# One fp32 product for the mean square, its eps folded into the sums; two products of constants at the start

## The chip, the cores and the metric

One core of a Trainium2 chip runs the kernel. The metric is the device time of one execution in microseconds (us). Five engines work side by side, each in its own order: TensorE (PE; its weight loads are listed as PEld), VectorE (DVE), ScalarE (ACT), GpSimd (POOL) and SyncE (SP), which here only issues DMAs.

## The reference

A layer over 2048 tokens of width 1024, all float32:

```python
h = rmsnorm(x, g_attn); p = h @ w_in            # 1024 x 2816
y_a = a_b * conv3(a_c * a_h)                    # 256 wide
y_b = silu(layernorm(conv31(glu) + b_conv_b))   # 256 wide
y_c = stick_breaking_attention(q, k, v)         # 8 heads of 64
x = x + concat(y_a, y_b, y_c) @ w_out
x = x + relu(rmsnorm(x, g_ffn) @ w_ff1)**2 @ w_ff2   # 4096 wide
return rmsnorm(x, g_final)

def rmsnorm(x, g):
    return x * rsqrt(mean(x * x, -1) + 1e-6) * g
```

## The kernel before, in words

Everything is kept transposed: features on the 128 partitions, tokens along the free dimension, in blocks of TB = 512 tokens. Each large product is made of three (`mm3`): operands are split into a rounded high part and a rest, high x high, rest x high and high x rest are summed in PSUM. The splits are made on ScalarE (the high part) and VectorE or GpSimd (the rest).

First part: `consts` and `attention_consts` fill constant tiles, among them `d1` (128x512, zeros with a one in every 32nd column, two fills on VectorE, lines 195 and 196), and load `g_attn`. `p_start` then loads the first 512 tokens of x and the first two units of `w_in`, and multiplies them as they come: for each of the 8 pieces d, `make_h` loads x, makes the high part `xh` (ScalarE, line 229) and the rest `xl` (VectorE, line 230), squares the piece (`x_square`: ScalarE, then an add on VectorE into `ss`) and yields; the two units' weights are split every second d; then the products of this d are issued (lines 317 to 319). After the first block `vectors` loads seven small vectors on SP's queue, `norm_x` makes R, the reciprocal root of the mean square spread over the partitions, and the results leave PSUM multiplied by R (`p_evac`, line 341 for the first). The second block of 512 tokens follows in the same way with one unit, and then `p_half` twice with all units, `mixer_b` and the first attention groups woven in.

Second part: four times `block`, one for each 512 tokens. It multiplies by w_out and adds x (`x2`), keeping `acc` (8 tiles), `hh` and `hl` (acc times g_ffn, split) and `ss`, the sum of squares. The FFN is computed on the values that are not yet normalised, so that its result has to be divided by the mean square m (plus eps); instead `acc` is multiplied by m and the last norm, which doesn't depend on a common factor, has its eps multiplied by m squared. For that `block` sums `ss` over the partitions with four fp32 products into a `z` bank (`colsum`, `ps_ss`), makes `mt` and `em` on VectorE, spreads `mt` over the partitions with four more fp32 products (`spread`, `ps_R`), and multiplies the eight `acc` tiles (line 1008). In the profile an fp32 product is two records. After that `ffn1` and `ffn2` alternate (32 pieces and 8 groups), the last group's results are squared into `ss2` (`square_sum`), and `finish_` makes the last norm from `ss2` with `em` as its eps. Attention of the next 512 tokens is woven into the first three blocks; its score tiles (`ps_z`, line 528) share the three `z` banks, and its chain on VectorE ends at T (line 656), on whose result further products wait. In the last block the final group runs in two halves of 256 tokens, and the first half's `finish_` is put into the second.

A planner orders the instructions of each engine's queue: it walks the program in its order, with some parts at higher priority (`high_priority`), and uses its own estimates of when each can start.

Of the kernel before, what the change touches and what calls it, by code (L numbers as in the profile page):

```python
# [7 lines left out]
F32 = mybir.dt.float32  # L8
F32R = mybir.dt.float32r
I32 = mybir.dt.int32  # L10
AF = mybir.ActivationFunctionType
# [4 lines left out]
P = 128  # L16
# [12 lines left out]
RMS_EPS = 1e-6  # L29
LN_EPS = 1e-5  # L30

UNITS = ["G0", "G1", "A0", "A1", "A2", "K0", "K1", "Q0", "Q1", "V0", "V1"]


def f(ap):
    return ap.bitcast(F32)
# [32 lines left out]
class Trunk:  # L69
# [39 lines left out]
    def rsqrt(self, ss, scale, eps, cols=slice(0, 4)):  # L109

        nc, pool = self.nc, self.tiny
        y = pool.tile([P, 4], F32, name="rs_y", tag="rs_y", bufs=6)
        v = pool.tile([P, 4], F32, name="rs_v", tag="rs_v")[:, cols]
        if isinstance(eps, float):
            nc.vector.tensor_scalar(v, ss[:, cols], scale, eps, op0=ALU.mult, op1=ALU.add)
        else:
            nc.vector.scalar_tensor_tensor(v, ss[:, cols], scale, eps[:, cols], op0=ALU.mult, op1=ALU.add)  # L117
        nc.gpsimd.tensor_tensor(y[:, cols], v, self.mhalf[:, cols], op=ALU.pow)  # L118
        return y
# [23 lines left out]

    def small(self, name, bufs=2):
        return self.tiny.tile([P, 4], F32, name=name, tag=name, bufs=bufs)


    def consts(self, ctx):
        nc, tc, a = self.nc, self.tc, self.a
        c = self.c = ctx.enter_context(tc.tile_pool(name="consts", bufs=1))  # L150
        self.tiny = ctx.enter_context(tc.tile_pool(name="tiny", bufs=2))
        self.dr = ctx.enter_context(tc.tile_pool(name="dr", bufs=1, space=DRAM))
        self.gvec = {}
        t = c.tile([P, DC], F32, name="g_attn")
        nc.scalar.dma_start(t, a["g_attn"].rearrange("(d p) -> p d", p=P))
        self.gvec["g_attn"] = t

        self.ident = c.tile([P, P], F32, name="ident")
        make_identity(nc, self.ident)
        self.ones2 = c.tile([P, 2], F32, name="ones2")  # L160
        nc.vector.memset(self.ones2, 1.0)
        self.mhalf = c.tile([P, 4], F32, name="mhalf")
        nc.vector.memset(self.mhalf, -0.5)
        self.KQ = self.dr.tile([H // 2, 2, P, 3, 2, S // 2], F32, name="KQ")
        self.VS = self.dr.tile([H, S, 2 * HD], F32, name="VS")
        self.Y = self.dr.tile([D, S], F32, name="Y")

        self.WS = self.dr.tile([len(UNITS), 2, P, DC, 256], F32, name="WS")


        self.split_w = {n: self.dr.tile([k, 2, P, 2, DC // 2, P], F32, name="s_" + n) for n, k in (("w_out", DC), ("w1", FC))}
        self.split_w["w2"] = self.dr.tile([FC // G, DC // 2, P, 2, G, 2, P], F32, name="s_w2")

    def vectors(self):
        nc, tc, a, c = self.nc, self.tc, self.a, self.c
        self.vb = {}
        for name in ("g_ffn", "g_final"):
            t = c.tile([P, DC], F32, name=name)
            self.dma(t, a[name].rearrange("(d p) -> p d", p=P))
            self.gvec[name] = t  # L180
        c = self.pc
        self.wa = c.tile([P, 2, 3], F32, name="wa")
        self.dma(self.wa, a["w_conv_a"].rearrange("(c p) k -> p c k", p=P))
        self.wb = c.tile([P, 2, 31], F32, name="wb")
        self.dma(self.wb, a["w_conv_b"].rearrange("(c p) k -> p c k", p=P))
        for name in ("b_conv_b", "ln_b_g", "ln_b_b"):
            t = c.tile([P, 2], F32, name=name)
            self.dma(t, a[name].rearrange("(c p) -> p c", p=P))
            self.vb[name] = t
# [27 lines left out]
    def make_h(self, hf, tb):  # L217

        nc = self.nc
        g = 2 * hf + tb  # L220
        ss = self.mx.tile([P, TB], F32, name="ss", tag="ss", bufs=2) if hf == 0 else None
        for d in range(DC):
            t = self.rp.tile([P, TB], F32, name="xraw", tag=self.rt, bufs=self.rb)
            self.dma(t, self.a["xT"][d * P : (d + 1) * P, g * TB : (g + 1) * TB])
            gv = self.gvec["g_attn"][:, d : d + 1]
            hi = self.xp.tile([P, TB], F32R, name=f"xh{tb}_{d}", tag=f"xh{tb}", bufs=DC)
            lo = self.xp.tile([P, TB], F32R, name=f"xl{tb}_{d}", tag=f"xl{tb}", bufs=DC)
            self.xh[tb][d], self.xl[tb][d] = hi, lo
            nc.scalar.activation(hi, t, AF.Copy, scale=gv)
            nc.vector.scalar_tensor_tensor(lo, t, gv, f(hi), op0=ALU.mult, op1=ALU.subtract)  # L230
            if hf == 0:
                self.x_square(ss, t, d, nc.vector)
            yield d
        if hf == 0:
            self.ss[g] = ss
# [67 lines left out]
    def p_start(self):  # L303

        nc = self.nc
        ws = [self.w_steps(0), self.w_steps(1)]
        for tb, units in ((0, (0, 1)), (1, (0,))):
            xs = self.make_h(0, tb)
# [523 lines left out]

    def square_sum(self, ss, t, d):
        nc = self.nc
        if d == 0:
            nc.scalar.activation(ss, t, AF.Square)
# [17 lines left out]
    def block(self, tb, before):  # L854
# [107 lines left out]
        def ffn2(g, cols=slice(0, TB), ahead=0, again=0):  # L962
# [13 lines left out]
            for d in range(DC):  # L976
# [12 lines left out]
                elif g == FC // G - 1:  # L989
                    self.square_sum(ss2[:, cols], acc[d][:, cols], d)  # L990
                yield 0.65 * G
# [4 lines left out]
        need2(1)  # L996

        mt = self.small("mt")
        nc.vector.tensor_scalar(mt, self.colsum([ss], "z"), 1.0 / D, RMS_EPS, op0=ALU.mult, op1=ALU.add)
        em = self.small("em")  # L1000
        nc.vector.scalar_tensor_tensor(em, mt, RMS_EPS, mt, op0=ALU.mult, op1=ALU.mult)
        yield from ffn1(2)
        need2(2)
        ms = self.spread(mt, "z")
        for d in range(DC):
            if d == DC // 2:
                yield from ffn1(3)
            nc.vector.tensor_tensor(acc[d], acc[d], ms, op=ALU.mult)
        ss2 = hp.tile([P, TB], F32, name="ss2", tag="ss", bufs=1)
        sq7 = []  # L1010
# [8 lines left out]
        if tb < 3:  # L1019
            self.attend(tb + 1)  # L1020
            self.y_load(tb + 1, self.y_order(tb + 1)[: self.xb])
            yield from ffn2(FC // G - 1, ahead=2)
            self.end = self.finish_(tb, acc, [ss2], em)
        else:

            left, right = slice(0, TB // 2), slice(TB // 2, TB)
            yield from ffn2(FC // G - 1, left)
            fin = self.finish_(tb, acc, [ss2], em, left)
            with self.tc.high_priority(offset=HP):
                for n, _ in enumerate(ffn2(FC // G - 1, right, again=1)):  # L1030
                    for _ in range(LEFT[n]):
                        next(fin, None)
            self.finish(tb, acc, [ss2] + sq7, em, right)
            for _ in fin:
# [6 lines left out]

    def finish_(self, tb, acc, sums, em, cols=slice(0, TB)):
        nc, a, hp = self.nc, self.a, self.hp
        ts = slice(tb * TB + cols.start, tb * TB + cols.stop)
        bs = range(cols.start // P, cols.stop // P)
        b = slice(bs[0], bs[-1] + 1)
        y = self.rsqrt(self.colsum(sums, "z", bs), 1.0 / D, em, b)
        yield
# [106 lines left out]
```

## Time and profile before

| what | us |
|---|---|
| median of 3 runs | 2396.55 (2396.35 to 2400.49) |
| the profiled execution's own time | 2399.65 |
| its span, first to last instruction | 2397.6 |
| TensorE busy | 2372.1 (99%) |
| VectorE, ScalarE, GpSimd busy | 1513.9, 1066.5, 1138.9 |

Rows of the profile give the start and the length of an instruction or of a run of them ("x8"). TensorE's matmuls overlap each other, so that the distance from one start to the next says more than the length. "Idle before" in square brackets is how long the engine had waited and what ended it.

### The profile page before, as it was taken

To read this page: it belongs to the slowest core of one execution; us is meant where nothing else is said; L and a number is where in the kernel's file an instruction comes from. 1 tells how busy PE (TensorE), PEld (TensorE's weight loads), DVE (VectorE), ACT (ScalarE), POOL (GpSimd) and SP (SyncE) were. 2 spreads that over 40 slices of the span, in tenths; PEclk is the share of its full clock that TensorE was granted. 3 is DMA by queue.
4 is the path that set the end of the run, shared out by engine and by line. 5 is a ranking of instruction groups with operands and counts; after the bars stand their busy time and mean duration, and the time that the engine had idled before them with its cause. 6 is when DMAs were issued, how large, how long until landed. Compare 5 with 4: busy or idle time off the path is not lost.

```text
span 2397.6 us, 32859 instructions
## 1 busy us (share of the span) xinstructions
PE 2372.1 (99%) x11316; PEld 2003.4 (84%) x11316; DVE 1513.9 (63%) x2500; ACT 1066.5 (44%) x2002; POOL 1138.9 (48%) x1223
## 2 busy tenths in 40 slices
PE   8999999999999999999999999999999999999998
PEld 7888988898887888888888888788888888888887
DVE  7966698833878777768766668586666625322114
ACT  5232443333566566545555555355555522311221
POOL 1342397732576666526666665278878710000000
PEclk9999999999999999999999999999999999999999
DMA  7569897789687777696676876766676556545545
GB/s 253 209 229 344 292 324 237 258 258 279 187 238 214 221 216 214 199 286 180 214 226 221 241 240 206 267 172 179 193 202 197 181 176 224 181 166 194 205 168 193
DMA packets 236677, 532.28 MB, mean 222 GB/s; under 512 B 26848, under 2 KB 100576, under 8 KB 221152
## 3 DMA queue, kind: packets, MB, share of 16 engines
q1 hardware_dynamic: 178000, 457.82, 57.0%
q0 software_dynamic: 39424, 62.93, 11.8%
q10 hardware_dynamic: 19088, 9.44, 1.4%
q8 instruction: 89, 1.46, 0.3%
q14 instruction: 76, 0.62, 0.1%
HBM read 381.99 MB, written 139.72 MB: 218 GB/s over the span
## 4 chain that ended last, share of the span: by engine, by line
PE 86%; DMA 5%; DVE 3%; issue 3%; POOL 2%; ACT 1%; SPq 0%; POOLq 0%; DVEq 0%; ACTq 0%
PE ps_y L103 9%; PE ps_y L105 9%; PE ps_y L107 9%; PE ps_u L107 9%; PE ps_u L103 9%; PE ps_u L105 9%; PE ps_p L107 4%; PE ps_p L105 4%; PE ps_p L103 4%; PE ps_z L528 3%; PE ps_z L529 3%; PE ps_o L735 2%; PE ps_o L734 2%; PE ps_o L726 2%; PE ps_x L103 2%
## 5 line engine op out<-in xcount | busy, mean ns | idle before, releaser
L90 POOL TENSOR_TENSOR Alo<-A,Ahi 128x512 fp32r<-128x512 f32 x288 | 385.1, 1346 | 101.0 <-ACT Ahi L88 68.1
L984 DVE TENSOR_TENSOR acc<-acc,ps_y 128x512 f32<-128x512 f32 (+1 forms) x264 | 175.8, 668 | 188.4 <-PE ps_y L107 186.4
L103 PE MATMUL ps_u<-hh,w 128*128 128x512 f32 x1024 | 280.0, 392 | 2.5 <-ACT hh L903 2.4
L103 PE MATMUL ps_y<-fh,w 128*128 128x512 f32 (+1 forms) x1056 | 281.7, 384 | 0.0
L105 PE MATMUL ps_y<-fh,w 128*128 128x512 f32 (+1 forms) x1056 | 280.3, 383 | 0.0
L107 PE MATMUL ps_y<-fl,w 128*128 128x512 f32 (+1 forms) x1056 | 279.4, 383 | 0.0
L623 POOL TENSOR_TENSOR A<-A,R 128x512 f32<-128x512 f32 x168 | 223.8, 1335 | 115.4 <-ACT A L621 93.8
L105 PE MATMUL ps_u<-hh,w 128*128 128x512 f32 x1024 | 277.5, 390 | 0.0
L107 PE MATMUL ps_u<-hl,w 128*128 128x512 f32 x1024 | 277.1, 390 | 0.0
L118 POOL TENSOR_TENSOR rs_y<-rs_v,mhalf 128x4 f32<-128x4 f32 (+1 forms) x13 | 13.2, 1018 | 482.3 <-DVE rs_v L117 437.0
L948 ACT ACTIVATE ps_u<-ps_u 128x512 f32<-128x512 f32 x128 | 74.5, 582 | 353.6 <-PE ps_u L107 349.0
L105 PEld LDWEIGHTS ps_y<-fh,w 128*128 128x128 f32 x1056 | 195.0, 188 | 39.6 <-DMA w<-wraw 0.3
L107 PEld LDWEIGHTS ps_y<-fl,w 128*128 128x128 f32 x1056 | 195.0, 188 | 38.9 <-DVE fl L958 0.2
L105 PEld LDWEIGHTS ps_u<-hh,w 128*128 128x128 f32 x1024 | 192.2, 188 | 40.5
L107 PEld LDWEIGHTS ps_u<-hl,w 128*128 128x128 f32 x1024 | 191.9, 188 | 39.9
L103 PEld LDWEIGHTS ps_y<-fh,w 128*128 128x128 f32 x1056 | 193.2, 188 | 36.8 <-DVE acc L984 0.2
L88 ACT ACTIVATE Ahi<-A 128x512 fp32r<-128x512 f32 x288 | 176.8, 625 | 105.2 <-PE ps_o L734 44.9
L103 PEld LDWEIGHTS ps_u<-hh,w 128*128 128x128 f32 x1024 | 187.6, 188 | 37.9 <-ACT hh L903 3.4
L958 DVE TENSOR_TENSOR fl<-ps_u,fh 128x512 fp32r<-128x512 f32 x128 | 87.9, 687 | 205.3 <-ACT fh L957 204.7
L90 DVE TENSOR_TENSOR w<-wraw,w 128x512 fp32r<-128x512 f32 x184 | 186.0, 1036 | 30.9 <-ACT w L88 29.8
L625 DVE TENSOR_TENSOR R<-ps_z,R 128x512 f32<-128x512 f32 x168 | 115.7, 689 | 129.3 <-ACT ps_z L622 105.2
L88 ACT ACTIVATE w<-wraw 128x512 fp32r<-128x512 f32 x184 | 110.3, 627 | 184.3 <-PE ps_y L107 126.6
(179 smaller groups left out, 4810.2 us busy)
## 6 DMA issues: line engine op xcount, KB each, us to landing
w<-s_w SPq DMA_DIRECT2D x200, 512.0 KB, 4.1
wraw<-in_w SPq DMA_DIRECT2D x224, 256.0 KB, 4.8
w<-s_w SPq DMA_DIRECT2D x52, 1024.0 KB, 4.8
w<-s_w_out SPq DMA_DIRECT2D x64, 512.0 KB, 4.9
s_w<-w SPq DMA_DIRECT2D x56, 512.0 KB, 4.7
s_w<-w SPq DMA_DIRECT2D x24, 1024.0 KB, 5.9
Qd<-KQ SPq DMA_DIRECT2D x64, 256.0 KB, 6.3
xraw<-in_xT SPq DMA_DIRECT2D x48, 256.0 KB, 5.1
```

The source lines that it names most:

```text
L88: nc.scalar.activation(hi, x, AF.Copy)
L90: e.tensor_tensor(lo, x, f(hi), op=ALU.subtract)
L103: self.nc.tensor.matmul(ps, wh, xh, start=start and k == 0, stop=False)
L105: self.nc.tensor.matmul(ps, wl, xh, start=False, stop=False)
L107: self.nc.tensor.matmul(ps, wh, xl, start=False, stop=stop and k == n - 1)
L528: nc.tensor.matmul(z[:, oc], keys, g["qh"][:, qc], start=k == 0, stop=False)
L529: nc.tensor.matmul(z[:, oc], keys, g["ql"][:, qc], start=False, stop=k == n - 1)
L623: nc.gpsimd.tensor_tensor(t, t, R, op=ALU.mult)
L625: nc.vector.tensor_tensor(Rn, z, R, op=ALU.mult)
L948: nc.scalar.activation(ps, ps, AF.Relu)
L958: nc.vector.tensor_tensor(lo, ps, f(hi), op=ALU.subtract)
L984: nc.vector.tensor_tensor(acc[d][:, cols], acc[d][:, cols], ps, op=ALU.add)
```

## The change

The diff's core, with all new functions and operands:

```diff
+EM = (D * RMS_EPS / P) ** 0.5
 def rsqrt(self, ss, scale, eps, cols=slice(0, 4)):
-        if isinstance(eps, float):
-            nc.vector.tensor_scalar(v, ss[:, cols], scale, eps, op0=ALU.mult, op1=ALU.add)
-        else:
-            nc.vector.scalar_tensor_tensor(v, ss[:, cols], scale, eps[:, cols], op0=ALU.mult, op1=ALU.add)
+        nc.vector.tensor_scalar(v, ss[:, cols], scale, eps, op0=ALU.mult, op1=ALU.add)
 def consts(self, ctx):
-        nc.scalar.dma_start(t, a["g_attn"].rearrange("(d p) -> p d", p=P))
+        nc.scalar.dma_start(t, a["g_attn"])
+        self.mean_d = c.tile([P, P], F32, name="mean_d")
+        nc.vector.memset(self.mean_d, 1.0 / D)
+        self.em_eps = c.tile([P, 1], F32, name="em_eps")
+        nc.vector.memset(self.em_eps, EM * RMS_EPS)
 def vectors(self):
-            self.dma(t, a[name].rearrange("(d p) -> p d", p=P))
+            self.dma(t, a[name])
...
 def make_h(self, hf, tb):
+            yield d
             if hf == 0:
                 self.x_square(ss, t, d, nc.vector)
-            yield d
 def p_start(self):
         ws = [self.w_steps(0), self.w_steps(1)]
+        for _ in range(2):
+            nc.tensor.matmul(self.psum("ps_warm", "o"), self.d1[:, 0:P], self.d1, start=True, stop=True)
-    def square_sum(self, ss, t, d):
+    def square_sum(self, ss, t, d, begun=False):
-        if d == 0:
+        if d == 0 and not begun:
 def block(self, tb, before):
-                    self.square_sum(ss2[:, cols], acc[d][:, cols], d)
+                    self.square_sum(ss2[:, cols], acc[d][:, cols], d, begun=True)
         yield from ffn1(0, 1)
         need2(1)
-        mt = self.small("mt")
-        nc.vector.tensor_scalar(mt, self.colsum([ss], "z"), 1.0 / D, RMS_EPS, op0=ALU.mult, op1=ALU.add)
-        em = self.small("em")
-        nc.vector.scalar_tensor_tensor(em, mt, RMS_EPS, mt, op0=ALU.mult, op1=ALU.mult)
         yield from ffn1(2)
         need2(2)
-        ms = self.spread(mt, "z")
+        ms = self.psum("ps_ms", "z")
+        nc.tensor.matmul(ms, self.mean_d, ss, start=True, stop=True)
+        ss2 = hp.tile([P, TB], F32, name="ss2", tag="ss", bufs=1)
+        nc.scalar.activation(ss2, ms, AF.Square, bias=self.em_eps, scale=EM)
         for d in range(DC):
             if d == DC // 2:
                 yield from ffn1(3)
-            nc.vector.tensor_tensor(acc[d], acc[d], ms, op=ALU.mult)
-        ss2 = hp.tile([P, TB], F32, name="ss2", tag="ss", bufs=1)
+            nc.vector.scalar_tensor_tensor(acc[d], ms, RMS_EPS, acc[d], op0=ALU.add, op1=ALU.mult)
 def finish_(self, tb, acc, sums, cols=slice(0, TB)):
-        y = self.rsqrt(self.colsum(sums, "z", bs), 1.0 / D, em, b)
+        y = self.rsqrt(self.colsum(sums, "z", bs), 1.0 / D, 0.0, b)
```

One product of a tile filled with 1/1024 and `ss` gives the mean on every partition. ScalarE writes D eps m² / 128 into `ss2` before the squares are added to it, so that the sum over 128 partitions holds the eps of the last norm. The eight small vectors come in the order of the partitions from the host, so that a partition's numbers are next to each other in memory. The first two products multiply `d1` with itself into a bank that nothing reads.

## Rows read from the trace of the kernel before

**Rows 1.** Busy time by stretch: start:end, length, each engine, clock, DMA share, GB/s

```profile
0.00:6.30 6.30, 0.00 (x0) 0.00 (x0) 1.43 (x8) 3.67 (x8) 1.31 (x8) 1.00 0.66 170
6.30:2386.30 2380.00, 2370.38 (x11304) 2001.94 (x11304) 1508.37 (x2482) 1062.39 (x1994) 1136.92 (x1214) 1.00 0.71 223
```

**Rows 2.** TensorE's waits: us in total, times, the longest

```profile
PE ps_z L528 <- DVE T L656: 6.6, 6, 1.6
...
PE ps_u L103 <- ACT hh L903: 2.4, 1, 2.4
```

**Rows 3.** Timeline of the first 13 us: start, length, instruction

```profile
0.81 0.48 ACTq L155 DMA_DIRECT2D g_attn<-in_g_attn  x1
...
1.72 0.07 DVE L196 MEMSET d<- 128x16 f32 x1
...
3.71 0.63 ACT L239 ACTIVATE ss<-xraw 128x512 f32<-128x512 f32 x1 [0.67 <-DMA xraw<-in_xT]
...
4.96 0.72 ACT L229 ACTIVATE xh<-xraw,g_attn 128x512 fp32r<-128x512 f32 x1 [0.62 <-DMA g_attn<-in_g_attn]
5.64 1.28 ACT L88 ACTIVATE wh<-wraw 128x512 fp32r<-128x512 f32 x2
...
6.32 2.08 PE L317 MATMUL ps_p<-xh,wh 128*128 128x512 f32 x4 [6.32 <-ACT wh L88]
...
10.63 0.69 DVE L90 TENSOR_TENSOR wl<-wraw,wh 128x512 fp32r<-128x512 f32 x1
...
12.39 0.39 PE L319 MATMUL ps_p<-xl,wh 128*128 128x512 f32 x1
```

**Rows 4.** The chain that ended last, at 50 and 228 us: start, length

```profile
50.31 1.81 PE ps_p L103 x8
...
227.74 1.72 PE ps_mean L467 x4
```

**Rows 5.** DMA issues of the first 30 us: size, us from issue to landing

```profile
g_attn<-in_g_attn ACTq DMA_DIRECT2D x1, 4.0 KB, 4.1
...
ln_b_g<-in_ln_b_g SPq DMA_DIRECT2D x1, 1.0 KB, 2.1
```

**Rows 6.** Timeline, the second block of x and the first norm

```profile
34.78 0.72 ACT L229 ACTIVATE xh<-xraw,g_attn 128x512 fp32r<-128x512 f32 x1 [3.86 <-DMA xraw<-in_xT]
...
38.54 1.28 DVE L341 TENSOR_TENSOR sig<-ps_p,R 128x512 f32<-128x512 f32 x2
...
43.30 0.84 PE L103 MATMUL ps_p<-xh,wh 128*128 128x512 f32 x3
```

**Rows 7.** Busy time of one stretch, while the vectors are loaded

```profile
14.20:18.80 4.60, 4.60 (x22) 3.79 (x21) 4.60 (x9) 3.99 (x8) 0.00 (x0) 1.00 0.55 49
```

**Rows 8.** Timeline of TensorE in the last block, around mt

```profile
2043.88 1.07 PE L107 MATMUL ps_u<-hl,w 128*128 128x512 f32 x4
2044.79 0.95 PE L127 MATMUL ps_ss<-ones,ss 128*128 128x2 f32 x8
2045.60 1.19 PE L103 MATMUL ps_u<-hh,w 128*128 128x512 f32 x4
2046.63 1.08 PE L105 MATMUL ps_u<-hh,w 128*128 128x512 f32 x4
...
2051.18 1.05 PE L134 MATMUL ps_R<-ident,mt 128*128 128x128 f32 x8
2051.99 1.18 PE L103 MATMUL ps_u<-hh,w 128*128 128x512 f32 x4
```

**Rows 9.** Groups of instructions by line and shape: busy us, mean ns, idle before

```profile
L622 ACT ACTIVATE ps_z<-ps_z 128x512 f32<-128x512 f32 x168 | 100.2, 596 | 0.0
...
L1008 DVE TENSOR_TENSOR acc<-acc,ps_R 128x512 f32<-128x512 f32 x32 | 19.7, 684 | 7.6 <-PE ps_R L134 7.6
...
L1054 DVE SCALAR_TENSOR_TENSOR ot<-acc,g_final,ps_R 128x512 f32<-128x512 f32 x24 | 17.7, 747 | 40.5 <-DMA outT<-ot 20.5 <-PE ps_R L134 19.7
...
L1001 DVE SCALAR_TENSOR_TENSOR em<-mt 128x4 f32<-128x4 f32 x4 | 4.0, 998 | 0.1
```

More of the change, by code (lines that the diff above doesn't have):

```diff
@@ L142, in psum_pool @@
         self.ps = ctx.enter_context(self.tc.tile_pool(name="ps" + str(banks["z"]), bufs=1, space=PSUM, reuse_waits="tile"))
-    def small(self, name, bufs=2):
-        return self.tiny.tile([P, 4], F32, name=name, tag=name, bufs=bufs)
     def consts(self, ctx):
@@ L182, in vectors @@
         self.wa = c.tile([P, 2, 3], F32, name="wa")
-        self.dma(self.wa, a["w_conv_a"].rearrange("(c p) k -> p c k", p=P))
+        self.dma(self.wa, a["w_conv_a"])
         self.wb = c.tile([P, 2, 31], F32, name="wb")
-        self.dma(self.wb, a["w_conv_b"].rearrange("(c p) k -> p c k", p=P))
+        self.dma(self.wb, a["w_conv_b"])
         for name in ("b_conv_b", "ln_b_g", "ln_b_b"):
             t = c.tile([P, 2], F32, name=name)
-            self.dma(t, a[name].rearrange("(c p) -> p c", p=P))
+            self.dma(t, a[name])
             self.vb[name] = t
@@ L1022, in block @@
             yield from ffn2(FC // G - 1, ahead=2)
-            self.end = self.finish_(tb, acc, [ss2], em)
+            self.end = self.finish_(tb, acc, [ss2])
         else:
@@ L1027, in block @@
             yield from ffn2(FC // G - 1, left)
-            fin = self.finish_(tb, acc, [ss2], em, left)
+            fin = self.finish_(tb, acc, [ss2], left)
             with self.tc.high_priority(offset=HP):
@@ L1032, in block @@
                         next(fin, None)
-            self.finish(tb, acc, [ss2] + sq7, em, right)
+            self.finish(tb, acc, [ss2] + sq7, right)
             for _ in fin:
@@ L1040, in finish, with finish_ @@
                 pass
-    def finish_(self, tb, acc, sums, em, cols=slice(0, TB)):
+    def finish_(self, tb, acc, sums, cols=slice(0, TB)):
         nc, a, hp = self.nc, self.a, self.hp
@@ L1136 @@
         ),
-        "g_attn": lay(np.asarray(inputs["g_attn"])[0]),
-        "w_conv_a": lay(np.asarray(inputs["w_conv_a"])[0].T),
-        "w_conv_b": lay(np.asarray(inputs["w_conv_b"])[0].T),
-        "b_conv_b": lay(np.asarray(inputs["b_conv_b"])[0]),
-        "ln_b_g": lay(np.asarray(inputs["ln_b_g"])[0]),
-        "ln_b_b": lay(np.asarray(inputs["ln_b_b"])[0]),
-        "g_ffn": lay(np.asarray(inputs["g_ffn"])[0]),
-        "g_final": lay(np.asarray(inputs["g_final"])),
+        "g_attn": lay(np.asarray(inputs["g_attn"])[0].reshape(DC, P).T),
+        "w_conv_a": lay(np.asarray(inputs["w_conv_a"])[0].reshape(3, 2, P).transpose(2, 1, 0)),
+        "w_conv_b": lay(np.asarray(inputs["w_conv_b"])[0].reshape(31, 2, P).transpose(2, 1, 0)),
+        "b_conv_b": lay(np.asarray(inputs["b_conv_b"])[0].reshape(2, P).T),
+        "ln_b_g": lay(np.asarray(inputs["ln_b_g"])[0].reshape(2, P).T),
+        "ln_b_b": lay(np.asarray(inputs["ln_b_b"])[0].reshape(2, P).T),
+        "g_ffn": lay(np.asarray(inputs["g_ffn"])[0].reshape(DC, P).T),
+        "g_final": lay(np.asarray(inputs["g_final"]).reshape(DC, P).T),
     }
```

## Prediction

> **What bounds the kernel now.** I read the busy time by stretch first. From 6.30 to 2386.30 us TensorE is busy 2370.38 of 2380.00 us; it does nothing in the first 6.30 us [rows 1], and 11.3 us of the span lie behind. VectorE is busy 1508 us of that middle, ScalarE 1062, and the DMA engines move 223 GB/s. So the time is the start, plus TensorE's own work, plus 9.6 us of gaps in it, plus a tail. The list of TensorE's waits says what the gaps are: 6.6 us in six waits of attention's score products for VectorE's T (line 656), and 2.4 us in one wait at a block's start [rows 2]. An edit counts if it shortens the start, TensorE's instructions or one of these waits. What it does to VectorE, ScalarE or a DMA counts only where it becomes a new wait of TensorE.
>
> **The start.** In the timeline ScalarE has its first x tile at 3.71 us, squares it, then sits until 4.96 for g_attn, makes xh in 0.72 and the weights' high part from 5.64; the first product starts at 6.32 [rows 3]. The 15th product starts at 12.39, so the first fourteen took 6.07 us, 0.434 each, although the granted clock is given as 1.00 for the stretch [rows 1, 3]. Later eight products take 1.81 us, 0.226 each [rows 4]. That is TensorE at the lower of its two levels (1.2 GHz) until about 12.2 us and at the upper (2.4 GHz) afterwards: 0.208 us lost on each of 14.
>
> Three edits meet here.
>
> *g_attn in rows of eight numbers.* The old load of 1024 single numbers took 4.1 us to land; one of 256 pieces, ln_b_g, took 2.1 [rows 5]. From its issue at 0.81 that is 2.9 us, before the x tile: the wait for g_attn goes, and the x tile at 3.71 is late next. Then xh 0.72 and the weights' first half of 1.28, 0.64: operands at 5.07. If ScalarE still squares first (0.63), 5.70.
>
> *Two products of constants.* They need d1, whose last piece ends at 1.79 [rows 3]; two new fills on VectorE stand before it (0.2 us is my estimate), so they start at about 2.05. The nearest row for a 512-column fp32 product is ps_mean: four records, two products, 1.72 us [rows 4], so 0.86 each at the upper level and twice that at the lower: 3.4 us for both, end at 5.45. The first real product is queued behind them and waits for the later of 5.45 and its operands. I take 5.5, which is 0.8 us earlier than now (bounds 5.1 and 6.3).
>
> *The clock.* Nothing of before shows how far products of constants bring the rise forward. If n of the fourteen still run slowly, the gain is 0.8 + (14 - n) x 0.208. Bounds: n = 14 gives 0.8, n = 0 gives 3.7. Now the engine runs about six microseconds at the lower level, from its first product on; with some 3.4 of these spent on constants about 2.6 are left, n = 6, gain 2.5. I take that.
>
> The rows show one such run-up. The Trainium skill (TensorE: Matmul & The Clock Gate, "What's actually happening") says that the default state is the throttled one, that activity releases it, and that one kernel had 6, 11 or 14 slow products from run to run. Its count of 11 would make the start's term 1.4 in place of 2.5 and the sum below 5.1 in place of 6.2. The single rise in the trace neither confirms nor denies the spread.
>
> Is TensorE fed when it comes earlier? Fourteen products done at 12.39 - 2.5 = 9.9 and ten more at 0.226 make 24 by 12.1, when it needs the second piece of both units' weights; VectorE finished that at 11.32 [rows 3]. Half a microsecond of slack, and the feed starts earlier too.
>
> *x_square behind the products, and the other vectors in rows.* The same squares and adds on the same engines, issued after the products of their d. Their cover is that the norm comes late: R is applied from 38.54 and TensorE takes the bank that this frees at 43.30 [rows 6]; one VectorE piece of 0.64 makes it free at 39.2, so 4.1 us of slack, 1.6 after TensorE moves up by 2.5. Nothing. The seven vector loads on SP's queue come ahead of the second x block; while their small pieces are moved the DMA engines deliver 49 GB/s from 14.20 to 18.80 us [rows 7], where 223 are the mean [rows 1]. In larger rows most of these 4.6 us come back. The second block's x is tight (ScalarE waits 3.86 us for it at 34.78 [rows 6]), so this is the cover for the 2.5 us by which TensorE comes earlier; without it up to 2.5 would be given back. I count 0 for it.
>
> **The norm in each of the four blocks.** Removed: ps_ss (8 records) and ps_R from mt (8 records). In the last block ps_ss starts at 2044.79 and the next products at 2045.60, 0.81; those four take 1.03 where four take 0.91 (2043.88 to 2044.79), so 0.12 more: 0.93. The spread: 2051.18 to 2051.99, 0.81 again, and about the same behind it: 0.92 [rows 8]. Together 1.85. Added: one fp32 product of 512 columns, 0.86 by ps_mean, 0.98 with the same loss behind it. Gain 0.87 to 0.99 a block; 0.93 x 4 = 3.7 us. TensorE had nothing else to do there, so it counts in full.
>
> VectorE: eight multiplications a block become scalar_tensor_tensor, 0.747 for 0.684 [rows 9]: +2.0 us over the kernel. d = 0 of the last sums gets an add of its own: by the same row 0.684 in three blocks and two halves in the last, +2.7. em goes (four of 1.00 [rows 9]), and mt: -4.0 at least. Net some +0.7 on an engine that is 63% busy: nothing. ScalarE: a Square of 128x512 from PSUM, 0.596 [rows 9], four times; it is 45% busy. A z bank is held as long as ps_R's was, plus that Square and 0.5 us; ps_ss no longer takes a turn in the ring. Nothing either way. If this cover fails it shows as waits at line 528, below. In the tail the extra add comes at d = 0, far ahead of the last sum: nothing.
>
> **Sum.** 2.5 + 3.7 = 6.2 us. The profiled execution took 2399.65 (span 2397.6), so 2393.45 on its scale; the median of the runs is 2396.55, 3.1 lower, so 2390.4.
>
> **Rivals.**
> *The start gives little.* The clock rises no earlier, or TensorE meets the second block's x and waits. For it: only 0.8 is sure if n = 14, and the x tiles are tight. Against: the constants keep the engine busy from 2.05, and DMA time is freed. 0.8 + 3.7 = 4.5 us: 2392.0, within 0.2%.
>
> *New waits of the score products (the other side).* The engines' queues are in an order that a planner lays out from its own costs, and the edits change what it starts from. The place is line 528 behind line 656: six waits now, 1.1 us each, out of 48 crossings in the second half (24 groups of heads and blocks, two each). VectorE's eight multiplications stand in its queue as one run, now 6.0 us for 5.5, and T can land behind them. Six more waits make +6.6 and cancel the gain (2397.0); from eleven more, +12, it is slower by over 0.2% (2402). For it: the waits exist, and they all lie in the first block. Against: the second block has the same crossings and TensorE waits for none there, and VectorE's load hardly changes.
>
> *The product of 512 columns is no cheaper.* If it cost 1.85, 2.5 would be left: 2394.0. Against it is the ps_mean row; I give it 3 in 100, inside the first rival's share.
>
> **How the numbers follow.** About 0.2%, 4.8 us, is what a measurement of this kernel can tell from no change. Forecast, start and norm both pay: 0.62, faster. The start, or a term of the norm, gives little: 0.18, same. New waits: 0.20, of which 0.13 cancel part or all of it (same) and 0.07 reach slower. So 0.62, 0.31, 0.07. Range: low end, n = 0 and operands at 5.1 (4.1), norm 4.0, and half of the six waits gone (3.3): 11.4, so 2385. High end: start 0.8 and norm 3.5 less three new waits (3.3) make 1.0: 2395.5. The forecast's own range is 2386 to 2391.7.
>
> **What the profile after would show.** A product of d1 with itself from about 2 us; the first real product near 5.5; spacing 0.226 from before 10 us. The g_attn load landing in about 2 us, and no stretch of 49 GB/s at 14 us. In each block one run of two ps_ms records, 0.86 to 0.98 us start to start, in place of two runs of eight. TensorE's busy time about 3.7 us less, apart from the 3.4 of constants and what the clock gives. The waits at line 528 near 6.6 us. Wrong if the real products start after 6.3 or stay slow to 12, if ps_ms takes over 1.5 us, if TensorE waits at 25 to 43 us, or if the waits at 528 grow past 12 us.

## The result, and the profile after

The median of 22 executions is 2403.1 us, of 22 of the kernel before beside them 2398.63: ratio 1.0017 [1.0009, 1.0025], 0.17% slower. That is inside the 0.2% that the prediction calls "same" by its size, though the interval excludes 1, and 7.6 us above the range's upper end; 2.1 of these lie in the kernel before, which measured 2398.63 here and 2396.55 when the prediction counted from it. One execution of the changed kernel took 8491.6 us (and one of e10, below, 6162.39); the ratios leave these out. The profiled execution took 2404.84, its span 2403.1, 5.5 more than the profiled one of before. Lines below the first edits have moved by 2: 528 is 530, 656 is 658, 462 is 464 and 467 is 469.

First the start, which answers to [rows 3]: the timeline of TensorE, start, length, instruction.

```profile
1.98 4.21 PE L308 MATMUL ps_warm<-d 128*128 128x512 f32 x4 [1.98 <-DVE d L196]
5.66 1.30 PE L319 MATMUL ps_p<-xh,wh 128*128 128x512 f32 x2
7.26 0.73 PE L319 MATMUL ps_p<-xh,wh 128*128 128x512 f32 x2 [0.30 <-ACT wh L90]
7.83 0.40 PE L320 MATMUL ps_p<-xh,wl 128*128 128x512 f32 x1
```

The constants run from 1.98 and the first real product starts at 5.66. The first two real products are slow, the two from 7.26 take 0.57 together, and from 7.83 on the distance is 0.23: three that are slow in whole or in part, where [rows 3] had fourteen slow ones. Next, the list of TensorE's waits, as in [rows 2]: us in total, times, the longest.

```profile
PE ps_z L530 <- DVE T L658: 7.0, 5, 2.4
PE ps_mean L469 <- ACT cb L464: 4.3, 1, 4.3
...
PE ps_u L105 <- DVE fl L960: 1.4, 1, 1.4
...
PE ps_z L530 <- DVE R L627: 0.8, 1, 0.8
```

The second line is new, and it is one wait of 4.3 us. Its place, in the timeline of TensorE at 118 us, of the kernel before and then of the changed one:

```profile
119.98 1.98 PE L107 MATMUL ps_p<-xl,wh 128*128 128x512 f32 x8
121.80 0.72 PE L127 MATMUL ps_ss<-ones,ss 128*128 128x2 f32 x6
122.38 1.96 PE L467 MATMUL ps_mean<-cb,avg 128*128 128x512 f32 x4
```

```profile
117.70 1.98 PE L109 MATMUL ps_p<-xl,wh 128*128 128x512 f32 x8
119.52 0.28 PE L126 MATMUL ps_ss<-ones,ss 128*128 128x2 f32 x2
124.06 3.78 PE L469 MATMUL ps_mean<-cb,avg 128*128 128x512 f32 x4 [4.26 <-ACT cb L464]
127.63 1.28 PE L126 MATMUL ps_ss<-ones,ss 128*128 128x2 f32 x6
128.77 3.76 PE L105 MATMUL ps_p<-xh,wh 128*128 128x512 f32 x8
132.33 2.35 PE L107 MATMUL ps_p<-xh,wl 128*128 128x512 f32 x8
```

Read the eight rest products ahead of the mean product (`ps_mean`): 119.98 became 117.70, so 2.28 us of the start have come this far. In both kernels 480 `ps_p` products stand ahead of that mean product in the queue. Its operand `cb` was there at 119.0 before (ScalarE's timeline), 3.4 us ahead of TensorE; now it comes at 124.0. Behind the wait eight products take 3.56 us instead of 1.81. The view of busy time by stretch (length, then busy us of PE, PEld, DVE, ACT and POOL, then the granted clock, DMA share, GB/s) shows why:

```profile
110.00:120.00 10.00, 9.80 (x45) 8.07 (x43) 9.93 (x16) 0.67 (x4) 1.29 (x1) 1.00 0.87 327
120.00:130.00 10.00, 5.94 (x13) 3.69 (x14) 8.30 (x14) 3.45 (x7) 1.26 (x1) 0.64 0.27 81
130.00:140.00 10.00, 10.00 (x43) 8.23 (x43) 2.67 (x7) 2.42 (x4) 2.56 (x2) 0.85 0.91 338
```

The granted clock is 0.64 and 0.85, between its two levels because it was at the lower one for part of each stretch. The second mean product starts 6.5 us later than before (234.06 against 227.58): from 2.3 early to 6.5 late, 8.8 us lost, 4.3 in the wait and 4.5 in slow products (TensorE has no other wait between the two mean products).

Why `cb` is late. ScalarE's timeline, before and after:

```profile
100.09 0.63 ACT L241 ACTIVATE xraw<-xraw 128x512 f32<-128x512 f32 x1 [4.36 <-DMA xraw<-in_xT]
100.63 2.18 ACT L88 ACTIVATE wh<-wraw 128x512 fp32r<-128x512 f32 x4
105.29 0.64 ACT L241 ACTIVATE xraw<-xraw 128x512 f32<-128x512 f32 x1 [2.48 <-DMA xraw<-in_xT]
...
118.41 0.60 ACT L462 ACTIVATE cb<-ps_c 128x512 f32<-128x512 f32 x1 [0.40 <-DVE ps_c L458]
```

```profile
101.51 0.63 ACT L241 ACTIVATE xraw<-xraw 128x512 f32<-128x512 f32 x1 [4.63 <-DMA xraw<-in_xT]
106.25 0.63 ACT L241 ACTIVATE xraw<-xraw 128x512 f32<-128x512 f32 x1 [4.11 <-DMA xraw<-in_xT]
106.79 2.18 ACT L90 ACTIVATE wh<-wraw 128x512 fp32r<-128x512 f32 x4
...
123.41 0.60 ACT L464 ACTIVATE cb<-ps_c 128x512 f32<-128x512 f32 x1 [2.84 <-DVE ps_c L460]
```

Line 241 squares x of the later blocks (a side stage, `x_norms`), each square behind its own load. Counted with the others of the first part, the squares shown are the 23rd and the 24th. The four high parts `wh` stood ahead of the 24th square; now they stand behind it and start at 106.79 instead of 100.63. VectorE's timeline shows who waits for them:

```profile
103.14 0.68 DVE L357 TENSOR_TENSOR ac<-ps_p,R 128x512 f32<-128x512 f32 x1
107.44 1.36 DVE L92 TENSOR_TENSOR wl<-wraw,wh 128x512 fp32r<-128x512 f32 x1 [3.61 <-ACT wh L90]
108.73 0.74 DVE L460 SCALAR_TENSOR_TENSOR ps_c<-g,wb,ps_c 128x512 f32<-128x512 f32 x1
```

VectorE stands idle for 3.61 us at the rest `wl`, with the 31-tap convolution (line 460) queued behind it, whose end is `cb`. From 45 to 125 us VectorE has 7.1 us of such waits, in three places; before it had none of that kind.

The norm, TensorE's timeline in block 0, in place of the two runs of eight in [rows 8]:

```profile
618.07 1.08 PE L109 MATMUL ps_u<-hl,w 128*128 128x512 f32 x4
618.99 1.02 PE L1003 MATMUL ps_ms<-ss,mean_d 128*128 128x512 f32 x2
619.45 1.49 PE L105 MATMUL ps_y<-fh,w 128*128 128x512 f32 x4
620.78 1.08 PE L107 MATMUL ps_y<-fh,w 128*128 128x512 f32 x4
```

0.46 to the next start, and the four behind it take 1.33 where four take 0.91: 0.88. Last, the vectors' stretch, as in [rows 7], and the whole middle, as in the second line of [rows 1]:

```profile
14.20:18.80 4.60, 4.60 (x22) 3.81 (x21) 4.60 (x8) 4.60 (x9) 0.00 (x0) 1.00 0.56 135
```

```profile
6.30:2386.30 2380.00, 2364.06 (x11204) 1994.36 (x11203) 1508.41 (x2465) 1060.01 (x1995) 1137.08 (x1214) 1.00 0.70 222
```

135 GB/s instead of 49. TensorE's idle time in the middle is 15.9 us instead of 9.6.

The path of the difference, from starts in TensorE's timeline (after minus before): -2.3 at 119 us; +6.5 at the second mean product; +5.5 at the fourth (475.0 against 469.5), where before had waits of its own; +8.90 at the last `ps_y` of block 0; then +7.95, +6.96, +5.57 at the last `ps_y` of blocks 1 to 3. So the norm gave 0.95, 0.99 and 1.39 us in three blocks, and block 0 lost 3.4. Two losses, then: one at 120 us, one in block 0. In block 0 the waits for T hardly grew (7.0 us for 6.6); with those for `fl` and R it makes 9.2 us of idle time, 2.6 more than before. The rest is the clock, here behind a wait of 2.40 us for T at 723.54 (stretch 720 to 730):

```profile
720.00:730.00 10.00, 7.60 (x29) 6.03 (x28) 8.18 (x18) 4.46 (x9) 4.22 (x6) 0.83 0.54 183
```

If block 0 gains 0.9 as its neighbours do, 3.4 + 0.9 - 2.6 = 1.7 us went into slow products; that is an estimate.

### The profile page after: what moved, and what is told of

Its sections match the earlier page's. It is cut to its first block, busy times and chain, and to the rows that moved or that the text cites. A ratio compares the mean times of both kernels' runs of the same rounds, so it can differ in the third digit from the quotient of the medians.

```text
span 2403.1 us, 32741 instructions
## 1 busy us (share of the span) xinstructions
PE 2375.6 (99%) x11264; PEld 2002.8 (83%) x11264; DVE 1520.0 (63%) x2499; ACT 1065.4 (44%) x2006; POOL 1139.1 (47%) x1223
## 4 chain that ended last, share of the span: by engine, by line
PE 86%; DMA 5%; DVE 4%; issue 2%; ACT 1%; POOL 1%; SPq 0%; POOLq 0%; DVEq 0%; ACTq 0%
PE ps_y L105 9%; PE ps_y L107 9%; PE ps_y L109 9%; PE ps_u L109 9%; PE ps_u L107 9%; PE ps_u L105 9%; PE ps_p L105 4%; PE ps_p L107 4%; PE ps_p L109 4%; PE ps_z L530 3%; PE ps_z L531 3%; DMA xraw<-in_xT 3%; PE ps_x L109 2%; PE ps_x L105 2%; PE ps_x L107 2%
```

## The experiments

Theory: the ordered queues take the gain back at these two places. First rival: the loss is the price of one of the edits itself (the constants, the later squares, the norm's instructions). Second: the waits are the draw of each execution.

**Which half?** Three kernels: the start's edits alone (e3), the norm's alone (e4), and the whole change without the constants (e5).

```diff
 # e3: before, with vectors in rows, the yield ahead of x_square, and
+        for _ in range(2):
+            nc.tensor.matmul(self.psum("ps_warm", "o"), self.d1[:, 0:P], self.d1, start=True, stop=True)
 # e4: before, with the hunks of rsqrt, square_sum, block and finish_
+        nc.tensor.matmul(ms, self.mean_d, ss, start=True, stop=True)
 # e5: after
-        for _ in range(2):
-            nc.tensor.matmul(self.psum("ps_warm", "o"), self.d1[:, 0:P], self.d1, start=True, stop=True)
```

> The kernel before with the start's three edits alone (vectors in rows, squares behind the products, two products of constants); the norm as before. Theory A: TensorE comes about 4 us early to 58 us, waits for the conv chain and loses the clock as in the changed kernel: 5 to 8 us slower than before, ratio 1.002 to 1.0035. Theory B: 4 us faster, ratio 0.998.

> The kernel before with the norm's edits alone. Theory A: nothing moves up to 550 us, 0.9 us is won in each block and between 0 and 5 us are given back in the first block's waits: ratio 0.9985 to 1.0005. Theory B: slower than before by 4 us or more.

> The changed kernel without the two products of constants. Theory A: TensorE comes some 2.5 to 3 us later to the conv chain, the wait at ps_mean is shorter by that, 1 to 2 us, which may or may not let the clock fall: between 6 us faster than the changed kernel (clock kept) and 1 us slower. Theory C: no wait, no fall of the clock, and the time before less 4 us.

Measured: e3 1.0004 [0.9995, 1.0012], e4 0.9989 [0.9981, 0.9998], e5 0.9988 [0.9979, 0.9997]. None has the early loss: the wait at `ps_mean` is 0.84 us in e3, 0.3 in e4 and in e5, and the clock from 120 to 130 us is 1.00. In all three the `wh` splits stand ahead of the 24th square. So neither half makes the loss alone. The early loss that was expected of e3 (1.002 to 1.0035) and the wait of 1 to 2 us expected of e5 did not come; e4 is in its range. e3 starts as early as the full change (its 470th `ps_p` product at 117.0 us, 119.3 before) and yet its median is not lower than that of before.

**Can the wait be taken away by moving the mean product?** Edit e1 asks for it two turns of its side stage later.

```diff
-            for _ in range(3):
+            for _ in range(5):
                 yield 1.8
             mean =
...
-            for _ in range(4):
+            for _ in range(2):
```

> The changed kernel, with the product that takes the mean in mixer_b issued two steps of that side later, and two steps fewer before its spread. Theory A (TensorE, now early, waits in its queue for VectorE's conv chain; the wait of 4.3 us and the slow clock behind it cost about 10.6 us in all between 58 and 130 us): no wait of over 1 us at ps_mean, the granted clock stays at 1.00 from 110 to 150 us, and the time falls by 9 to 11 us against the changed kernel, to about 0.9975 of the kernel before. Theory B (the loss comes from the blocks: the product, the multiplications, new waits of the score products): the time moves by less than 3 us. Theory C (the clock falls at 124 us whatever TensorE does, as a late price of the constants): the wait goes and the clock still falls; gain about 4 us.

Measured: 1.0019 [1.0008, 1.003]. The edit did not do what it was for: the planner left 480 products ahead of the first mean product and moved the fourth instead (1704 products ahead of it for 1656). The wait was 3.88 us and the clock 0.62, so it is only a second showing of the loss.

**Does the order in ScalarE's queue make the wait?** In part. e10 and e11 spread the side stage of the squares a little later, so that the 24th square falls behind the `wh` splits again; e12 does the opposite in the kernel before; e13 is the changed kernel once more.

```diff
 # e10: after (e11: 68, 188; e12: before, with 56, 176)
-(Side(self.x_norms()), 24, 60, 180, True)
+(Side(self.x_norms()), 24, 64, 184, True)
```

> The changed kernel with one number altered: the side that squares the third and fourth x block in the first half (x_norms) runs from 64 to 184 of the main steps in place of 60 to 180. In ScalarE's queue this puts the 24th square of x behind the four splits of the next unit's weights, as it stood in the kernel before; TensorE's place for ps_mean is unchanged (480 products of ps_p ahead of it). Theory A1 (the conv chain is late because VectorE waits for weight splits that stand in ScalarE's queue behind a square that waits for its x load): cb is ready at 117 to 120 us and not at 124, the wait at ps_mean is under 1.5 us, the clock stays at 1.00 between 110 and 150 us, and 8 to 10 us are won against the changed kernel: ratio 0.996 to 0.9985. Theory A2 (TensorE simply arrives 2 to 3 us too early at a chain whose time is fixed): a wait of 3 us or more stays, with the fall of the clock. Theory B (blocks): under 3 us.

> The same with 68 to 188: the same place of the 24th square in ScalarE's queue, later squares further back, and ps_mean two products later in TensorE's queue. Theory A1: as the other one, within 3 us of it. A2 and B as there.

> The kernel before with the same side from 56 to 176, which puts the 20th and the 24th square ahead of the weight splits in ScalarE's queue, as in the changed kernel; none of the change's edits. Theory A1: the conv chain is late by 4 to 5 us (cb at 123 to 124 us), TensorE, which comes to ps_mean at about 122, waits 1 to 2.5 us, and the time grows by 1 to 9 us according to whether the clock falls. Theories A2 and B: no wait of over 0.5 us at ps_mean, time within 2 us of the kernel before.

> The changed kernel once more, unaltered. All theories: ratio 1.0005 to 1.003. Theory A1: again a wait of 3.5 to 5 us at ps_mean and a granted clock under 0.9 from 120 to 130 us, since the queues' order is the same in each execution. The wait total of the score products in the first block, 9.2 us in the first profile, comes out within 3 us of that if the order sets it, anywhere between 5 and 15 if the memory's timing does.

Measured, on one chip: e13 1.0022 [1.0011, 1.0032] (wait 3.44), e10 0.9996 [0.9982, 1.001], e11 1.0037 [1.0025, 1.005], e12 1.0002 [0.9992, 1.0012]. e10's line in the timeline of TensorE, and its clock:

```profile
122.27 1.98 PE L469 MATMUL ps_mean<-cb,avg 128*128 128x512 f32 x4 [1.32 <-ACT cb L464]
```

```profile
120.00:130.00 10.00, 8.68 (x40) 6.62 (x39) 8.36 (x14) 4.03 (x8) 1.28 (x1) 1.00 0.31 91
```

With the wait at 1.32 us the clock stays at 1.00, and e10 is 0.0026, some 6 us, faster than the changed kernel beside it; 8 to 10 were expected. But the order alone did not do it. The edit shifts the whole side stage: the 23rd square, the last one ahead of the splits as in the kernel before, came only at 104.46, and the splits start at 104.99 where they started at 100.63. VectorE still waits 3.57 us for them (its timeline, 105.64), and `cb` came at 122.2, not at 117 to 120. Of the 2.9 us by which the wait is shorter than the changed kernel's 4.26, 1.8 are the earlier `cb` and 1.2 a later TensorE (its 470th product at 118.2 for 117.0).

e11, expected within 3 us of e10, is some 10 us slower. It has no wait at `ps_mean` either (`cb` at 120.7), but two others, which end at 337.18 (2.11 us, `ps_o` behind ScalarE's Ahi) and 363.47 (3.93, `ps_z` behind VectorE's R). No square stands in ScalarE's queue near 337; how the shift makes them isn't shown.

e12 did not set up what it was for. Its 24th square stands ahead of the splits, but its squares all come earlier, and the splits start at 100.41, as before; VectorE does not wait for them. `cb` came at 121.0, not at the 123 to 124 expected, and 2 us later than before because ScalarE copied it behind a square that had waited 2.77 us for its load (ScalarE's timeline, 119.81), and TensorE came to the mean product only at 123.2. So e12 says nothing on the order of the splits.

Over all the profiles the order does divide them. In the five kernels with the changed kernel's order (after, e1, e13, e15, e16) the splits start at 105.9 to 107.4 and `cb` comes at 123.1 to 124.5; in the eleven with the splits ahead of the 24th square they start at 99.3 to 105.0 and `cb` comes at 117.6 to 122.2, e10 last in both.

**Which edit made that order?** e15 puts the squares back ahead of the yield in the changed kernel; e16 is the norm's edits and the constants alone.

```diff
 # e15: after
-            yield d
             if hf == 0:
                 self.x_square(ss, t, d, nc.vector)
+            yield d
 # e16: e4, and
+        for _ in range(2):
+            nc.tensor.matmul(self.psum("ps_warm", "o"), self.d1[:, 0:P], self.d1, start=True, stop=True)
```

> The changed kernel with the square of x put back ahead of the yield; rows, constants and the norm's edits stay. In ScalarE's queue the 24th square of x still stands ahead of the weights' splits, as in the changed kernel. Theory (that order is the cause, whichever edit made it): the wait at ps_mean stays at 3 to 4.5 us at about 119.8, the clock falls behind it, ratio 1.001 to 1.0025. Rival (the square's move itself is the cause): the wait goes to under 1.5 us, ratio 0.999 or less.

> The kernel before with the norm's edits and the two products of constants alone; the vectors and the squares of x as in the kernel before. In the written order this pair already puts the 24th square of x ahead of the weights' splits in ScalarE's queue; neither edit does so by itself. Theory (this order makes the wait, through the square's late x tile): cb after 122.5 us, a wait of 2.5 to 4.5 us at ps_mean near 120, ratio 1.0005 to 1.0025. Rival (the wait needs the rows or the moved squares as well, through the DMA queue): cb at 118 to 120.5, wait under 1 us, ratio 0.9975 to 0.999.

Measured: e15 1.002 [1.0008, 1.0031], wait 3.47: the moved squares are not the cause. e16 1.0007 [0.9996, 1.0018], in the range, but with a wait of 1.35 us for the 2.5 to 4.5 expected: `cb` came as late as foreseen (124.5), and TensorE came late too, its 470th product at 120.4. Without the rows its first real product started at 6.43, ten real products ran slowly in spite of the constants (0.43 apart to 10.87), and it waited 1.4 us for the `g` of line 353. The clock stayed at 1.00. So the loss takes the late `cb` and the early TensorE together. In e16's queue as in the full change's the square stands first; with only one of its two edits it does not. The norm's edits lie 500 us behind that place in time, and still they decide there, through the planner.

**Is it the profiled execution alone?** The record lists the mean granted clock of every execution. Its mean is 0.9981 over 133 executions of the kernel before and 0.9965 over 21 of the changed kernel; 0.9960 to 0.9962 in e13, e15 and e1, which share its early wait; 0.9964 in e11 with its two late ones; 0.9970 to 0.9977 in e3, e4, e5, e10, e14, e16 and e17; 0.9979 to 0.9982 in e12 and in e18 to e20, below. At the lower level, half of the upper one, as much time is lost as the mean falls short of 1. So, as an estimate, 0.0016 x 2400 us = 3.8 us is what the lower level costs the changed kernel's executions beyond those of before.

**And block 0?** e14 (norm and rows, without constants) and e17 (norm alone, once more) keep the old order at 120 us.

> The kernel before with the norm's edits and the vectors in rows; no constants, squares of x issued before the yield as in the kernel before. In ScalarE's queue the weights' splits stand ahead of the 24th square of x, as in the kernel before. Theory (the loss of the full change is the one wait at ps_mean that this order makes, and the clock behind it): no wait over 1.5 us at ps_mean, granted clock 1.00 from 120 to 130 us; norm alone gave 2.6 us, rows bring the first operands about 0.6 to 1.3 earlier, so 3 to 4 us faster than before, ratio 0.9985. Rival (an earlier TensorE meets the waits of the first block instead and gives the start back): no faster than the norm alone, ratio 0.9989 or above, and more waits between 550 and 1030 us than the 11.7 us lost there before.

> The kernel with the norm's edits alone, once more, unaltered. Its first comparison gave 0.9989 [0.9981, 0.9998], 2.6 us. Theory (each of the four blocks loses the difference of the products, 0.9 us, and nothing is given back): 0.9985 to 0.999. Rival (the first number was luck of the first block's waits): 0.9995 or more, with more idle time of TensorE at the score products than before.

Measured: e14 0.9998 [0.9988, 1.0009], e17 0.9998 [0.9986, 1.001]. No wait at `ps_mean`, clock 1.00 there, as expected; but the gain that was expected of e14 isn't there, and e4's 0.9989 did not come again in the same program (e17; the intervals overlap). Both profiles lose it in block 0. e17, timeline of VectorE, then of TensorE:

```profile
749.44 0.73 DVE L640 STREAM_TRANSPOSE ps_t<-R 128x512 f32<-128x512 f32 x1
754.63 0.69 DVE L92 TENSOR_TENSOR w<-wraw,w 128x512 fp32r<-128x512 f32 x1 [4.47 <-ACT w L90]
755.24 1.21 DVE L642 TENSOR_TENSOR_SCAN T<-d,ps_t 128x512 f32<-128x512 f32 x1
...
759.04 2.62 DVE L92 TENSOR_TENSOR w<-wraw,w 128x512 fp32r<-128x512 f32 x1
...
762.05 0.69 DVE L659 TENSOR_TENSOR T<-T,ps_t 128x512 f32<-128x512 f32 x1
```

```profile
762.80 0.58 PE L531 MATMUL ps_z<-Qd,Kd 128*128 128x256 f32 x1 [4.33 <-DVE T L659]
...
764.46 1.90 PE L105 MATMUL ps_u<-hh,w 128*128 128x512 f32 x4
766.16 1.12 PE L107 MATMUL ps_u<-hh,w 128*128 128x512 f32 x4
```

It resembles the first loss. The scan that makes T stands in VectorE's queue behind the rest of a weights' split, which waits for ScalarE's high part, which waits 6.59 us for its load (ScalarE's timeline, 753.97). A second rest stands between the scan and T and takes 2.62 us. TensorE's score product waits 4.33 us for T, and the four products behind it take 1.70 instead of 0.91; the granted clock from 760 to 770 is 0.83. In the kernel before this scan, the 16th, stands elsewhere in VectorE's queue (32 rests of `w` ahead of it, 35 in e17), and the longest wait for T is 1.6 [rows 2].

But the place of the scan does not set the price. In e4, the same program, the scan waits almost as long; the second rest is short, and TensorE waits 1.14 us. VectorE's timeline of e4:

```profile
752.80 0.69 DVE L92 TENSOR_TENSOR w<-wraw,w 128x512 fp32r<-128x512 f32 x1 [4.19 <-ACT w L90]
...
757.21 0.91 DVE L92 TENSOR_TENSOR w<-wraw,w 128x512 fp32r<-128x512 f32 x1
```

Why the same rest takes 0.91 or 2.62 us isn't shown. In the changed kernel the scan at this place waits behind a rest for 2.73 us and the second rest takes 3.54, for a wait of 2.29; ahead of the wait of 2.40 at 723.54 the scan itself did not wait, and a rest of 3.10 us stands between it and T. The draw has a part in it: e13 is the changed program once more, its score waits were expected within 3 us of 9.2, and all its waits in block 0 came to 5.3.

**Only the blocks where it pays.** e18 keeps the norm's edits to blocks 1 to 3; VectorE's queue is then that of before to the end of block 0 but for three small fills, and ScalarE's and GpSimd's are the same instruction for instruction. e20 adds the vectors in rows. e19 is the whole change with block 0 left as before and the squares at 64 to 184.

```diff
 # e18: before, with the norm's hunks under a condition
+        if tb == 0:
+            ms = self.spread(mt, "z")
+        else:
+            ms = self.psum("ps_ms", "z")
+            nc.tensor.matmul(ms, self.mean_d, ss, start=True, stop=True)
```

> The kernel before with the norm's edits in blocks 1 to 3 only; block 0 computes its norm as before, and VectorE's queue is the one of before up to the end of block 0. Theory (in block 0 the norm's edits put the scan for T behind a weights' split that waits for its DMA, and that takes back what the other three blocks give): from the fourth mean product to the end of block 0 538 to 540 us as in the kernel before, blocks 1 to 3 0.9 to 1.2 us shorter each, in all 3 us, ratio 0.9985 to 0.999. Rival (the first block's waits are the draw of each execution, whatever the order): 541 to 545 us there, ratio 0.9993 or more.

> The changed kernel with two things undone: block 0 keeps its norm of before, and the stage that squares x is spread over 64 to 184 instead of 60 to 180, so that the 24th square stands behind the weights' splits. Theory (two places ate the gain and both are mended): wait at ps_mean under 1.5 us, clock 1.00 from 120 to 130 us, block 0 at 538 to 540 us, in all 2.3 - 1 + 3 = 4 to 5 us faster than before, ratio 0.998 to 0.9985. Rival (a TensorE that is 2 us earlier meets other waits between 120 and 1030 us): 0.9992 or more.

> The kernel before with the vectors in rows and the norm's edits in blocks 1 to 3; no constants, squares as before. Theory: 0.8 us from the start and 3 us from the norm, ratio 0.998 to 0.9988. Rival (the earlier start is lost in block 0's waits): 0.9992 or more.

Measured, on one chip: e18 0.9985 [0.9976, 0.9994], 2394.31 us; e19 0.9984 [0.9974, 0.9993], 2393.29; e20 0.9986 [0.9977, 0.9995], 2394.62; the kernel before 2397.39. All three came out in the ranges of their theories, 2.8 to 4.1 us below the kernel before; the changed kernel, 0.17% and 0.22% slower than before in its own comparisons, was not run beside them. The waits of e18:

```profile
PE ps_z L534 <- DVE T L662: 5.0, 6, 1.4
```

All profiles by the same measure, starts in TensorE's timeline, in us (block 0 from the fourth mean product to its last `ps_y`, blocks 1 to 3 from there to the last `ps_y` of block 3; e1 has its fourth mean product elsewhere):

| kernels | block 0 | blocks 1 to 3 |
|---|---|---|
| block 0 with the old norm: before, e3, e12 | 539.4, 538.3, 539.9 | 1377.0, 1376.3, 1375.8 |
| norm's edits in all blocks: after, e13, e15, e16 | 542.8, 539.3, 541.8, 544.5 | 1373.7, 1373.3, 1373.5, 1371.7 |
| the same: e4, e17, e14, e5, e10, e11 | 539.3, 543.3, 544.8, 544.9, 539.7, 544.5 | 1373.9, 1372.3, 1372.6, 1371.7, 1374.7, 1373.4 |
| block 0 old, the others edited: e18, e19, e20 | 537.6, 537.4, 536.9 | 1372.5, 1372.4, 1372.9 |

Blocks 1 to 3 gain 3.3 us on the mean of the second and third line (1373.1 against 1376.4), 1.1 a block. Block 0 with the edits takes 542.5 on the mean against 539.3, from nothing to 5.6 us more, the same program included (e4 and e17: 539.3 and 543.3). That rules out a fixed price. It is not a draw whatever the edits are either: the six profiles with the old block 0 lie between 536.9 and 539.9, the ten with the edits between 539.3 and 544.9. By itself the draw is worth some 2 us: e18 has the queues of before and took 1.8 less. The clock divides them too. By stretches of 10 us, the granted clock falls below 1.00 in block 0 in ten of the eleven profiles with the edits there (all but e10), and in none of the six others.

In e19 the start gave only 0.5 us by its 470th product (118.8 against 119.3). Its constants ran from 1.98 like the changed kernel's, but ScalarE had to wait for the load of the first weights until 6.40, the first real product started at 7.08, and seven real products ran slowly (0.43 apart to 10.23, TensorE's timeline). So it doesn't test whether the full 2.3 can be kept, and e16 and e19 show that two products of constants do not always bring the rise forward.

## Why the prediction was wrong

**The start: the size was right,** in part by luck. 2.5 predicted, 2.3 measured at 119 us; the first real product at 5.66 for 5.5, spacing 0.23 from 7.83. `g_attn` landed in 3.2 us, not 2.1, but before xh needed it. The count was wrong: three real products ran slowly, not six. Three would make 0.66 + 11 x 0.208 = 2.9; a wait of 0.30 for the second unit's split and first products that were further apart than 0.43 took the difference. The Trainium skill's spread of slow products (TensorE: Matmul & The Clock Gate, "What's actually happening"), by which the start's term could have been 1.4, shows in the runs: without constants 14 in the kernel before and 13 in e12, 7 in e18, and 9 and 13 in e4 and e17, one program; with constants 2 to 4 in seven profiles, 7 in e19 and 10 in e16.

**The norm: the size was right, in three blocks.** One product costs 0.88, 0.46 of it up to the next start and the rest in the four products behind it; the gain is 0.95 to 1.39 a block.

**The failed step is the sum,** "2.5 + 3.7 = 6.2 us", with the two covers that carried it. "1.6 after TensorE moves up by 2.5. Nothing", on the slack of the first norm, held where it looked, TensorE's feed up to 43 us, and looked no further; the sum then carried the 2.5 to the end. The next place where TensorE meets another engine's chain is the mean product at 122 us, with 3.4 us of slack in the kernel before. That slack alone would have covered 2.3 (e3, as early and with the old order, waits 0.84); but the edits also moved the planner's order, `cb` came 5 us later, and the wait and the clock took 8.8. And "Net some +0.7 on an engine that is 63% busy: nothing" is an average, and it put the norm's edits in block 0 at no cost: there 2.6 us of new waits and the clock behind them took the block's gain and 3.4 us more. The sum had no term for the clock after the start.

**The rivals.** The second one had the mechanism, "The engines' queues are in an order that a planner lays out from its own costs, and the edits change what it starts from", and named the first block, where the smaller loss is (3.4 us after, up to 5.6). Its sign, line 528 behind 656, hardly moved in the changed kernel (7.0 for 6.6); e17 and e14 have single waits of 4.33 and 4.54 there. It missed the larger place, and what a long wait costs through the clock, and it had only 0.20. The first (the start gives little) did not happen in the changed kernel; a start that gives little came in e16 and e19. The third (no cheaper product) did not happen.

**The list of signs.** Each named sign came out, bar the landing, the busy time and the form of the norm's product (0.46 from start to start, 0.88 only with the loss behind it), and none of the five "wrong if" did: the waits at 530 are 7.0. The list had only places that the argument had looked at.

**What stays open.** Why the start alone (e3) is no faster in its median, though its profiled execution, one of its fastest, ended 2.1 us earlier. And that it is the scan's place in VectorE's queue, not the dearer multiplications beside it, is read from rows: undoing block 0's edits undoes both, and e4 speaks against the place alone. Why two products of constants left three slow products in one kernel and ten in another.

## What to carry to other kernels

Where queues are laid out by a planner, price an edit twice: its own work, and the next places where TensorE takes a result of another engine's chain, each with its slack in the trace of before; time gained upstream is kept only as far as the first slack that is smaller. After such an edit compare the order of every engine's queue, also far from the edit, and look for an instruction that waits for a load (a weights' split) directly ahead of a chain that TensorE needs. If one instance of a repeated edit loses its gain to a new order, try leaving that instance out: the same edit in three of four blocks gave 0.9985 [0.9976, 0.9994], in all four 0.9989 [0.9981, 0.9998] and 0.9998 [0.9986, 1.001]. The intervals overlap; what separates the kernels is block 0 in their profiles.

## What the runs showed of the hardware

What a wait costs beyond itself isn't fixed by its length. TensorE's idle time at `ps_mean` and the granted clock of 120 to 130 us: 4.26 and 0.64 (after), 3.88 and 0.62 (e1), 3.44 and 0.83 (e13), 3.47 and 1.00 (e15), 1.35 and 1.00 (e16), 1.32 and 1.00 (e10). Waits of nearly the same length left the clock alone in e15 and lowered it in e13. Shorter waits in block 0 went either way too: behind 1.88 us (e17, at 658) and 2.18 (e4, at 719) the clock of the next 10 us was 0.83, behind 1.94 (e14, at 657) and 2.40 (e10, at 759) it was 1.00. The Trainium skill (TensorE: Matmul & The Clock Gate, "HAM oscillation — how this bites in real kernels") describes waits between bursts that bring the slow level back; the traces agree for the long waits (3.88 us and more), and show that those from 1.88 to 3.47 us can go either way.
